# Thirty-two matmuls of ones and the identity between the last norm's sums and the spread of its result

## The chip, the cores and the metric

The kernel runs on one core of a Trainium2 chip. The metric is the device time of one execution in microseconds (us), and less is better. Five engines take part: TensorE (PE, with its weight loads listed apart as PEld), VectorE (DVE), ScalarE (ACT), GpSimd (POOL) and SyncE (SP), the last of which issues most of the transfers (DMAs) from the memory of the chip.

## The reference

The input is one sequence of 512 frames with 1024 channels in float32. Two layers each do

```
x = x + 0.5 * swiglu(rms_norm(x, ffn1_norm), ffn1_w_in, ffn1_w_out)
x = x + hybrid_mixer(rms_norm(x, mix_norm), ...)   # conv | stick-breaking | retention
x = x + 0.5 * swiglu(rms_norm(x, ffn2_norm), ffn2_w_in, ffn2_w_out)
```

and after the second layer stands the last norm, with which the change has to do:

```
def rms_norm(x, g):
    y = x * lax.rsqrt(jnp.mean(x * x, axis=-1, keepdims=True) + 1e-6)
    return y * g
```

## The kernel before, in words

The activations lie transposed: eight tiles `x[d]` of 128 channels by 512 frames. Matrix products in float32 are made from matmuls in a reduced format (`F32R`): every operand is split into a high and a low part, and each product takes three matmuls (lines 432 to 434, and 658 to 660 for a scheme of blocks that needs seven block products for eight). Weights come from memory as raw tiles of 512 KB (`load`, line 387), ACT copies the high part (line 374), DVE subtracts it for the low part (line 377); some weights are split with the help of an accumulating DMA from POOL instead.

The order of the work is not written out by hand. Every operation is put on a list with an engine, a planned cost, its dependencies and a shift named `late`. A planner (`Plan.forward`) then steps through a planned time: whenever an engine is free, it takes the operation that is ready and has the lowest rank, where the rank is the operation's place on the list plus `late`. The resulting order is emitted, and on the chip each engine works through its own instructions in that order. Several shifts are given by name and by kind of stage (`SHIFTS`); in the first stage all that `weight` does, the loads of raw weights included, carries a shift of -1015. Only the order comes from the planned costs; on the chip the instructions wait for semaphores. On-chip buffers are taken from rooms with a fixed number of places; the banks of `mm` are three.

The start of the program (`run`, from line 1327 on) puts on the list, one after another: the load of the gains (`const`, line 1341), a small memset, `warm` (ten matmuls of zeros, line 600), then the loads of the `x[d]` (line 1355) with pieces of the first weights (`first_weights`, line 582) between them. The first product (lines 432 to 434, tile `pf`) needs the first `x` scaled by its gain (line 465) and a piece of the first weights.

The end is the last norm, `norm(self.y, True)`, and is a chain in which each step waits for the one before:

- ACT squares the last `x[d]` (line 474). The other squares were added up by DVE before.
- `sums` (line 551): TensorE sums the squares over the channels, eight small matmuls for the last `sq`, into the bank `ss`.
- `inv_sqrt`: DVE scales and adds the epsilon (line 488, tile `ms`), POOL raises to the power of -1/2 (line 495, tile `rt`).
- `spread`: DVE lays the 512 results on diagonals (line 518, tile `dg`), and TensorE multiplies them by ones, in full float32, into the bank `bc` (line 537). In the trace this matmul is two instructions.
- DVE multiplies each `x[d]` by gain and `bc` (line 1413), and SP sends the eight results out (line 1418).

## Time and profile before

| | |
|---|---|
| median of 3 runs | 1920.43 us (1914.89, 1920.43, 1923.8) |
| the profiled execution's own time | 1916.82 us |
| its span, from the first to the last instruction | 1915.1 us |
| TensorE busy (PE) | 1884.7 us, 98% of the span |
| weight loads (PEld) | 1683.5 us, 88% |
| VectorE, ScalarE, GpSimd busy | 69%, 50%, 12% |
| mean granted TensorE clock | 0.995 |
| read from memory | 288.98 MB |

The profile is one execution. In a timeline each row gives the start, the time from the first start to the last end of a merged group, the engine, the line of the program, the operation with its tiles (output, arrow, inputs), and behind `x` how many instructions were merged; in square brackets stands how long the engine had been idle and what ended that. A row of windows gives for a stretch of time the busy time of each engine with the number of instructions, the granted TensorE clock as a part of full speed (PEclk), the busy share of the DMA engines, and their rate. In the chain that ended last, each row is a start, a length and what the end of the program hung on in that time. The records of matmuls overlap, since matmuls are pipelined; the distance between two starts says how fast they follow each other.

### The profile page before, as it was taken

Reading aid. Unit: us, or ns where it says so; the run is one execution under the profiler, and the core shown is the slowest. Engines: PE = TensorE matmul, PEld = TensorE weight load, DVE = VectorE, ACT = ScalarE, POOL = GpSimd, SP = SyncE. Lnnn points to the kernel's source line nnn. Section 1 sums busy time; section 2 is a strip of 40 time slices with the busy share of each in tenths; the row PEclk is TensorE's granted clock in tenths of the full one; section 3 lists DMA queues with packets and bytes.
Section 4 is the critical chain, followed back from the end, with each engine's and each line's share of the span. In section 5 each row is a group of like instructions: output and inputs, shape, how many; then the busy total and the mean of one; then the engine's idle time right before and its main releaser. Section 6 shows DMA issues by size and latency. Waiting matters only on the chain.

```text
span 1915.1 us, 28971 instructions
## 1 busy us (share of the span) xinstructions
PE 1884.7 (98%) x11412; PEld 1683.5 (88%) x11412; DVE 1326.1 (69%) x1921; ACT 963.6 (50%) x1527; POOL 226.2 (12%) x262
## 2 busy tenths in 40 slices
PE   9999999999999999999999999999999999999997
PEld 7899999888878889899889999998888889998995
DVE  6865656699787856566685656657987887564665
ACT  5444444455886534343554444444668855353442
POOL 1011010011101010110211010100111020110100
PEclk9999999999999999999999999999999999999998
DMA  8457665465347577676866675655554385675742
GB/s 249 121 155 181 179 170 152 137 163 125 94 93 188 136 178 190 166 187 167 213 145 170 166 198 163 176 141 142 132 136 120 76 216 140 167 207 153 188 136 78
DMA packets 106343, 301.35 MB, mean 157 GB/s; under 512 B 12384, under 2 KB 13920, under 8 KB 106208
## 3 DMA queue, kind: packets, MB, share of 16 engines
q0 software_dynamic: 43520, 112.74, 30.6%
q1 hardware_dynamic: 62688, 186.78, 30.0%
q8 instruction: 89, 1.46, 0.3%
q14 instruction: 46, 0.38, 0.1%
HBM read 288.98 MB, written 2.10 MB: 152 GB/s over the span
## 4 chain that ended last, share of the span: by engine, by line
PE 81%; DVE 7%; DMA 7%; issue 2%; ACT 2%; SPq 0%; POOL 0%; POOLq 0%; DVEq 0%; ACTq 0%
PE po L432 8%; PE po L433 8%; PE po L434 8%; PE pu L658 6%; PE pu L660 6%; PE pu L659 6%; DMA w_raw<-in_f_in 5%; PE pr L660 4%; PE pr L658 4%; PE pr L659 4%; PE pf L432 4%; PE pf L433 4%; PE pf L434 4%; DVE yc L1198 2%; PE mo L433 2%
## 5 line engine op out<-in xcount | busy, mean ns | idle before, releaser
L377 DVE TENSOR_TENSOR w_lo<-w_raw,w_hi 128x1024 fp32r<-128x1024 f32 (+2 forms) x281 | 313.3, 1116 | 170.4 <-PE po L434 58.6
L374 ACT CAST w_hi<-w_raw 128x1024 fp32r<-128x1024 f32 (+2 forms) x281 | 269.6, 963 | 240.2 <-DMA w_raw<-in_f_in 71.9
L432 PE MATMUL po<-hh,w_hi 128*128 128x512 f32 x704 | 275.8, 392 | 0.3 <-DVE x L777 0.3
L433 PE MATMUL po<-hl,w_hi 128*128 128x512 f32 x704 | 275.4, 391 | 0.0
L434 PE MATMUL po<-hh,w_lo 128*128 128x512 f32 x704 | 273.9, 389 | 0.0
L658 PE MATMUL pr<-T_hi,s_hi 128*128 128x256 f32 x560 | 158.2, 282 | 2.6 <-ACT ga L695 2.6
L658 PE MATMUL pu<-B_hi,w_hi 128*128 128x256 f32 x560 | 158.5, 283 | 2.0 <-DVE up L708 1.9
L659 PE MATMUL pu<-B_lo,w_hi 128*128 128x256 f32 x560 | 158.4, 283 | 0.0
L660 PE MATMUL pu<-B_hi,w_lo 128*128 128x256 f32 x560 | 158.2, 283 | 0.0
L659 PE MATMUL pr<-T_lo,s_hi 128*128 128x256 f32 x560 | 158.2, 282 | 0.0
L660 PE MATMUL pr<-T_hi,s_lo 128*128 128x256 f32 x560 | 158.1, 282 | 0.0
L434 PEld LDWEIGHTS po<-hh,w_lo 128*128 128x128 f32 x704 | 132.2, 188 | 28.6
L432 PEld LDWEIGHTS po<-hh,w_hi 128*128 128x128 f32 x704 | 132.5, 188 | 24.4 <-DVE x L777 1.2
L433 PEld LDWEIGHTS po<-hl,w_hi 128*128 128x128 f32 x704 | 132.7, 188 | 22.2
L673 POOL DMA_DIRECT2D w_raw<-in_f_in x70 | 84.0, 1209 | 573.9 <-DMA w_raw<-in_f_in 409.3
L777 DVE SCALAR_TENSOR_TENSOR x<-po,x 128x512 f32<-128x512 f32 x128 | 87.0, 686 | 54.6 <-PE po L434 54.1
L402 ACT ACTIVATE w_lo<-w_hi 128x1024 fp32r<-128x1024 f32 (+2 forms) x85 | 79.3, 932 | 89.1 <-DMA w_hi<-in_f_out 19.6
L432 PE MATMUL pf<-xh,w_hi 128*128 128x512 f32 x304 | 119.1, 392 | 0.0
L434 PE MATMUL pf<-xh,w_lo 128*128 128x512 f32 x304 | 118.5, 390 | 0.0
L433 PE MATMUL pf<-xl,w_hi 128*128 128x512 f32 x304 | 118.4, 390 | 0.0
L721 ACT ACTIVATE ga<-ga 128x512 f32<-128x512 f32 x88 | 55.4, 630 | 120.2 <-DVE ga L715 109.3
L695 ACT COPY ga<-pr 128x256 f32<-128x256 f32 x140 | 51.7, 370 | 126.5 <-PE pr L660 125.8
(216 smaller groups left out, 5034.5 us busy)
## 6 DMA issues: line engine op xcount, KB each, us to landing
w_raw<-in_f_in SPq DMA_DIRECT2D x225, 512.0 KB, 4.6
w_raw<-in_f_in POOLq DMA_DIRECT2D x70, 512.0 KB, 7.8
w_raw<-in_f_out SPq DMA_DIRECT2D x48, 320.0 KB, 3.3
w_raw<-in_f_out SPq DMA_DIRECT2D x38, 384.0 KB, 4.0
w_raw<-in_m_in SPq DMA_DIRECT2D x26, 512.0 KB, 4.3
w_hi<-in_f_out POOLq DMA_DIRECT2D x26, 384.0 KB, 4.4
w_lo<-in_f_out POOLq DMA_DIRECT2D x26, 384.0 KB, 5.0
w_hi<-in_f_in POOLq DMA_DIRECT2D x19, 512.0 KB, 6.3
```

Of the source, the lines that this page charges most:

```text
L374: self.a(n, lambda: nc.scalar.copy(view(hi), view(src)), [src], [hi])
L377: lambda: nc.vector.tensor_tensor(out=view(lo), in0=view(src), in1=view(hi).bitcast(F32), op=ALU.subtract),
L402: self.a(n, lambda: nc.scalar.activation(lo[:, :n], hi[:, :n].bitcast(F32), ACT.Copy, scale=-1.0), [hi], [lo])
L432: mm(acc[:], hi[:, c], h[:], start=first and a + i == 0, stop=False)
L433: mm(acc[:], hi[:, c], l[:], start=False, stop=False)
L434: mm(acc[:], lo[:, c], h[:], start=False, stop=last and a + i == len(ks) - 1)
L658: mm(out, hi[:, c], h, start=first and j + i == 0, stop=False, **opts)
L659: mm(out, hi[:, c], l, start=False, stop=False, **opts)
L660: mm(out, lo[:, c], h, start=False, stop=j + i == 2, **opts)
L673: lambda: nc.gpsimd.dma_start(rs[:].rearrange("p (a b) -> p a b", a=2), src[:, None, 2 * q : 3 * q].to_broadcast([P, 2, q]), accum_op=ALU.add,
L721: self.last_silus = [self.a(S, lambda: nc.scalar.activation(g[:], g[:], ACT.Silu), [g], [g], "silu")]
L777: lambda x=x, po=po: nc.vector.scalar_tensor_tensor(out=x[:], in0=po[:], scalar=-0.5, in1=x[:], op0=ALU.mult, op1=ALU.add),
```

## The change

The change has four parts, all on what the program emits or on what the planner believes:

- `norm`, when it is the last, calls a new function `keep(8, ...)` after the sums. It takes a bank named `kept` from the room `mm` and emits 32 matmuls of 128 columns with `ones_r` as the weights and `ident_r` as the moving operand. Nobody reads the bank. The planner is told that the operation comes after the last sums.
- The load of the gains moves behind the load of `x[0]` on the list, and carries the shift `FIRST`, -20000.
- The planned cost of one matmul of `warm` goes from 0.6 to 0.5 us. The ten matmuls stay.
- Loads of the first weights and of `x` may carry the same shift up to a number `EARLY`. With `EARLY = 0` neither condition (`j < EARLY`, `d < 2 * EARLY - 1`) is met by any of them.

```
+FIRST, EARLY = -20000, 0
...
             self.pe(0.225 * TT, sums, [sq, self.ones], [ps])
+        if last:
+            self.keep(8, len(self.plan.ops) - 1)
         self.r = self.inv_sqrt(ps, TT, 1.0 / D)
         bc = self.spread(self.r, room, "bc", 1 if last else 2)
...
-        self.pe(0.6 * n, fn, [t], [ps])
+        self.pe(0.5 * n, fn, [t], [ps])
+
+    def keep(self, n, sums):
+
+        ps = self.bank(self.mm, "kept")
+
+        def fn():
+            for i in range(4 * n):
+                self.nc.tensor.matmul(ps[:, :P], self.ones_r[:], self.ident_r[:], start=i == 0, stop=i == 4 * n - 1)
+
+        self.pe(0.24 * n, fn, [self.ones_r, self.ident_r], [ps]).deps.add(sums)
...
-        gains = const("gains", [P, 3 * DEPTH + 1, KT])
-        g = [Col(gains, i) for i in range(3 * DEPTH + 1)]
         self.x = [self.tile(self.f2, f"x{d}") for d in range(KT)]
...
-            self.dma(262144, lambda: nc.sync.dma_start(x[:], io["x"][:, d, :]), [], [x])
+            self.dma(262144, lambda: nc.sync.dma_start(x[:], io["x"][:, d, :]), [], [x], FIRST if d < 2 * EARLY - 1 else 0)
...
+        load_x(0)
+        gains = const("gains", [P, 3 * DEPTH + 1, KT], late=FIRST)
+        g = [Col(gains, i) for i in range(3 * DEPTH + 1)]
...
         for j in range(4):
-            load_x(2 * j)
+            if j:
+                load_x(2 * j)
```

## The prediction

> **What bounds the kernel now.** I read the page first: the share of each engine, the granted clock, the chain that ended last.

> ```profile
> span 1915.1 us, 28971 instructions
> PE 1884.7 (98%) x11412; PEld 1683.5 (88%) x11412; DVE 1326.1 (69%) x1921; ACT 963.6 (50%) x1527; POOL 226.2 (12%) x262
> PEclk9999999999999999999999999999999999999998
> PE 81%; DVE 7%; DMA 7%; issue 2%; ACT 2%; SPq 0%; POOL 0%; POOLq 0%; DVEq 0%; ACTq 0%
> ```

> TensorE is busy for all but 30.4 us (1915.1 - 1884.7) and carries 81% of the chain. What is put behind its work, or delays its first product, therefore reaches the end one for one. The clock is whole in every slice but the last. So I went to the last 15 us, where the new matmuls go, with the timeline and then with windows of 1 us.

> ```profile
> 1899.62 0.69 DVE L777 SCALAR_TENSOR_TENSOR x<-po,x 128x512 f32<-128x512 f32 x1 [2.12 <-PE po L434]
> ...
> 1901.03 1.05 PE L551 MATMUL ss<-ones,sq 128*128 128x1 f32 x8 [1.45 <-ACT sq L474]
> 1902.12 0.16 DVE L488 TENSOR_SCALAR ms<-ss 128x4 f32<-128x4 f32 x1 [1.81 <-PE ss L551]
> 1902.43 1.04 POOL L495 TENSOR_TENSOR rt<-ms,mhalf 128x4 f32<-128x4 f32 x1 [34.50 <-DVE ms L488]
> 1903.50 0.69 DVE L518 TENSOR_TENSOR dg<-c_ident,rt 128x512 f32<-128x512 f32 x1 [1.22 <-POOL rt L495]
> ...
> 1904.34 2.05 PE L537 MATMUL bc<-dg,ones 128*128 128x512 f32 x2 [2.26 <-DVE dg L518]
> 1906.42 0.75 DVE L1413 SCALAR_TENSOR_TENSOR o<-x,c_gains,bc 128x512 f32<-128x512 f32 x1 [2.23 <-PE bc L537]
> ```

> ```profile
> 1903.00:1904.00 1.00, 0.00 (x0) 0.00 (x0) 0.50 (x1) 0.00 (x0) 0.47 (x1) 0.91 0.00 0
> 1904.00:1905.00 1.00, 0.66 (x1) 0.50 (x2) 0.19 (x1) 0.00 (x0) 0.00 (x0) 0.50 0.00 0
> 1905.00:1906.00 1.00, 1.00 (x2) 0.00 (x0) 0.00 (x0) 0.00 (x0) 0.00 (x0) 0.50 0.00 0
> ```

> The sums end at 1902.08. TensorE then has nothing until 1904.34, while DVE, POOL and DVE work. In that pause the clock falls to a half (0.91 of the third window: (1 - 0.91) / 0.5 = 0.18 us of it are low, so it fell near 1903.82), and `bc` runs for 2.05 us at the half clock. The eight `o` wait for it, and the outputs for them. The pause and the slow `bc` are all that the new matmuls can touch.

> **Part 1: the 32 matmuls.** They stand behind the sums and ahead of `bc` in TensorE's queue; `bc` is the only instruction behind them. How fast do they follow each other? The nearest rows are eight matmuls of the same size, with the same identity moving, and two of the same size in the scores:

> ```profile
> 508.84 0.22 PE L935 MATMUL z<-qh,kk 128*128 128x128 f32 x1
> 508.90 0.27 PE L935 MATMUL z<-ql,kk 128*128 128x128 f32 x1
> ...
> 511.49 1.00 PE L1129 MATMUL rbc<-ident_r,ex 128*128 128x128 f32 x8
> 512.33 0.45 PE L432 MATMUL pj<-xh,w_hi 128*128 128x512 f32 x1
> ```

> From the first of the eight to what comes after them are 0.84 us, so 0.105 us each; the pair stands 0.06 apart. I take 0.105: it is a run of eight with its weight loads, and 32 of them are a run too; 0.06, seen between two alone, is the lower bound. The matmul after the eight began 0.16 us before their end (511.49 + 1.00 - 512.33), so the first new one can begin at 1902.08 - 0.16 = 1901.92. 32 x 0.105 = 3.36 us, and `bc` begins at 1905.28 instead of 1904.34: 0.94 us later.

> What does `bc` gain? TensorE would now be busy from 1901.03 on, so I take the clock to stay whole. The same float32 product, 512 wide and in two instructions, at full clock:

> ```profile
> 497.54 1.02 PE L1102 MATMUL yce<-yr,c_centre 128*128 128x512 f32 x2
> ```

> So `bc` ends at 1906.30, and DVE starts 0.03 us behind it as before (1904.34 + 2.05 = 1906.39 against 1906.42): 1906.33, a gain of 0.09 us. What the clock gives, the queue takes back. Break-even is (1905.37 - 1901.92) / 32 = 0.108 us for one matmul; nothing is lost in the queue below (1904.34 - 1901.92) / 32 = 0.076. The price lies so near the break-even that the sign of this term is open, its size is not. Bounds: -1.03 us at 0.06 (rival 1), +2.04 us if the clock falls all the same (rival 2).

> [...]

> The bank costs no wait: the last reader of any `po` bank, the row at 1899.62, is done 1.6 us before. The operands are constants of the start. Nothing waits for the result.

> **Part 2: the gains go first.** SP's queue at the start, and the chain there:

> ```profile
> 0.74 0.86 SPq L387 DMA_DIRECT2D w_raw<-in_f_in  x2
> ...
> 1.64 0.43 SPq L1341 DMA_DIRECT2D c_gains<-in_gains  x1
> 2.12 0.47 SPq L1355 DMA_DIRECT2D x<-in_x  x1
> ```

> ```profile
> 1.18 4.98 DMA w_raw<-in_f_in
> ...
> 6.18 1.00 ACT w_hi L374
> ...
> 7.24 0.72 ACT xh L465
> 7.96 0.30 ACT wf_hi L374
> ...
> 8.30 0.50 PE pf L432
> ```

> Before, the two raw loads go ahead of the gains, since their rank carries -1015. With -20000 the gains pass both; `x[0]`, which is moved on the list as well, keeps a rank above theirs and stays fourth. The first three issues only change places, so `x[0]` still goes at 2.12 and all behind it as before. But the chain runs through the second raw load: it is issued one place later, 2.12 - 1.64 = 0.48 us. Its cast on ACT stands ahead of `xh`, which follows it at once, so the first product begins at 8.78. From there TensorE runs without a pause, so this term is +0.48 us. Lower bound 0, if the memory and not the issue sets when the load lands; below nothing only by the clock (next). 0.48 is the nearest row, and I take it.

> The clock has its own phase at the start:

> ```profile
> 9.00:10.00 1.00, 1.00 (x4) 0.70 (x4) 1.00 (x4) 1.00 (x3) 0.00 (x0) 0.71 1.07 381
> ...
> 12.00:13.00 1.00, 1.00 (x4) 0.78 (x3) 0.89 (x2) 1.00 (x4) 0.00 (x0) 0.59 1.00 365
> ```

> ```profile
> 10.13 0.43 PE pf L433
> ...
> 14.20 0.23 PE pf L433
> ```

> Some 3.4 us (0.58 and 0.82 us in these two windows, 2 between) run at half clock, a product of 0.23 us taking 0.43. That is 3.4 x (1 - 0.23 / 0.43) = 1.6 us which another execution may have or not: it widens the range by 1.6 us each way.

> **Part 3: `warm` at 0.5 us in the plan; `EARLY = 0`.** The matmuls stay, and on the chip TensorE idles between them and the first product:

> ```profile
> 1.46 4.63 PE L600 MATMUL warm<-zeros 128*128 128x512 f32 x10 [1.46 <-DVE mhalf L1358]
> 8.30 0.50 PE L432 MATMUL pf<-xh,wf_hi 128*128 128x512 f32 x1 [2.21 <-ACT wf_hi L374]
> ```

> A planned end that is 1 us earlier gives TensorE nothing that is ready, so I cost it at nothing; what hides it is the wait for `wf_hi`. `EARLY = 0` shifts no load: nothing.

> **Sum.** +0.48 - 0.09 = +0.39 us. Against the profiled execution: 1916.82 + 0.39 = 1917.2 us. That execution lies 3.6 us below the median of the three runs, and all four spread over 8.9 us, so I centre on their mean, 1918.99: 1919.4 us.

> **The rivals.**

> 1. *The pause holds the new matmuls.* At 0.06 us each they end at 1903.84, `bc` starts at 1904.34 as before and ends at 1905.36: -1.03 us, with the start 1918.99 - 1.03 + 0.48 = 1918.4 us. For it speaks the pair in the scores; against it the run of eight.

> 2. *The clock falls all the same.* If matmuls 128 wide do not count as work enough, 18 are done by 1903.82; below, a matmul goes from 0.12 to 0.21 us at the low clock, so the other 14 take 0.184 each, `bc` starts at 1906.4 and takes 2.05. DVE starts near 1908.46: +2.04 us, in all 1921.5 us. The change would then not do what it is for. [...]

> 3. *The other side: the planner writes another order, and loads come late.* In the plan the first raw loads start one place of SP later. The room of raw tiles has two places, so the third load waits for the split of the first and may lose its turn to a constant; each later pick of the planner depends on what is ready, and a swap at the start can be carried on. What one late load costs, this trace shows once in the first stage:

> ```profile
> PE pr L658 <- ACT ga L695: 2.2, 1, 2.2
> ```

> ```profile
> 150.39 0.12 PE pr L658
> ...
> 152.70 10.54 DMA w_raw<-in_f_in
> ...
> 166.93 0.21 PE pr L658
> ```

> ```profile
> 166.00:168.00 2.00, 1.86 (x9) 1.86 (x10) 2.00 (x4) 0.64 (x2) 0.00 (x0) 0.61 0.74 124
> 168.00:170.00 2.00, 2.00 (x12) 2.00 (x11) 2.00 (x3) 1.08 (x2) 0.00 (x0) 0.54 0.89 316
> ```

> A load of 10.54 us stops TensorE for 2.2 us, and 3.4 us of half clock follow (1.56 and 1.84 in the two windows), worth 3.4 x (1 - 0.12 / 0.21) = 1.5: 3.7 us. From three more such stalls on (11.1 us, 1930.5 us) the change is slower by more than 0.5%. Against it: all loads from `x[0]` on keep their place, and once TensorE is the bound a shift of all times alike changes no pick.

> 4. *The same, the other way*: an order that loses its stalls. Of TensorE's 30.4 us of idle time, 8.7 come after `bc`, 2.26 and 1.45 before it, 3.7 at the start; some 14 remain, of which 9.6 would have to go. About 1909 us.

> **How the numbers follow.** 0.5% is 9.6 us, about what a measurement of this kernel can tell from no change. The forecast has 0.64, rival 1 0.10, rival 2 0.08: all three lie within 2.5 us of the time before, so 0.82 for the same. Rival 3 has 0.12 and rival 4 0.06. The range: from the lowest run, less rival 1 (1.0), the clock at the start (1.6) and part of one stall, 1911; upward from the highest, plus 0.5, 2.0 and 1.6, 1928, and to 1930 to meet rival 3.

> **What the next profile would show.** On TensorE one group of 32 `kept` matmuls from about 1901.9 (plus the shift of the start), 3.4 us long; the clock at 1.00 until `bc` ends; `bc` x2 in 1.02 us, and DVE's first `o` within 0.2 us of where it was, counted from the sums' end. Distances near 0.06 show rival 1, a clock of 0.5 over `bc` rival 2. At the start the gains ahead of both raw loads, and the first product near 8.8. A plan that is unchanged shows the same groups and counts on every engine but for TensorE's 32; other stalls of TensorE, or changed splits of the work, show rivals 3 or 4. The prediction is wrong if the order moves: nothing in the two terms themselves can reach 9.6 us.

## The result, and the profile after

| | before | after |
|---|---|---|
| median of 22 runs each | 1920.43 us (1914.89 to 1928.61) | 1929.5 us (1924.64 to 1933.14) |
| the profiled execution's own time | 1916.82 us | 1925.42 us |
| its span | 1915.1 us | 1923.7 us |

The ratio is 1.0038, with a 95% interval from 1.003 to 1.0047: slower by about 7.3 us (5.8 to 9.0); the two medians lie 9.07 us apart. The median lies in the predicted range, near its upper end, and the step is smaller than the 0.5% that the forecast counted as no change. But the interval excludes no change: the term of the tail came out with the other sign and many times its size, and the planner's order, which the sum left out, cost as much again. Only the term of the gains came out about as forecast.

The page of the changed kernel hardly tells the two apart: the same counts on every engine but TensorE (32 more), the clock whole in every slice but the last, a chain that is TensorE's.

```profile
span 1923.7 us, 29021 instructions
PE 1891.6 (98%) x11444; PEld 1689.9 (88%) x11444; DVE 1326.7 (69%) x1921; ACT 965.3 (50%) x1527; POOL 226.4 (12%) x262
PEclk9999999999999999999999999999999999999998
PE 84%; DVE 7%; DMA 6%; ACT 2%; issue 1%; SPq 1%; DVEq 0%; ACTq 0%; POOLq 0%
```

**Where the 8.6 us of span are.** TensorE does the same matmuls in both kernels, so one can follow a tile by its k-th matmul. The tile `bc` of the norms gives the first and the last of twelve such points, before and then after (times are those of the first and the last start):

```profile
L537 PE MATMUL bc<-dg,ones_r x12: 392/393/500, 33.1 to 1562.4; 128*128 128x512 f32 x12
```

```profile
L539 PE MATMUL bc<-dg,ones_r x12: 392/393/505, 34.3 to 1567.3; 128*128 128x512 f32 x12
```

After lags by 1.2 us at 33 us and by 4.9 us at 1562 us. Matched matmul by matmul, the lag jumps to 8.59 us near 50 us, falls to 4.61 us near 170 us, wanders between 3.0 and 5.4 us from there, is 5.38 us at the last sums and 8.6 us at the end. So there are two losses, one in the first 60 us and one behind the last sums, and a part of the first is given back. Of the 1.2 us at 33 us, 0.6 are the later first product. The rest goes with the half clock of the start, where the products begin 0.43 us apart: it ends at 14.26 here and at 12.88 before, but at 14.42 in e1, which has the order of before, so it is not the change that moves it. (The clock's record of this trace begins at 14.25 us, so that its window rows show a whole clock ahead of that.)

**The tail.** The timeline of the changed kernel, with the windows of the same stretch (columns as in the prediction; the value behind POOL is the granted clock):

```profile
1906.41 1.05 PE L553 MATMUL ss<-ones,sq 128*128 128x1 f32 x8 [1.45 <-ACT sq L476]
...
1907.32 5.86 PE L616 MATMUL kept<-ident_r,ones_r 128*128 128x128 f32 x32
...
1908.88 0.69 DVE L520 TENSOR_TENSOR dg<-c_ident,rt 128x512 f32<-128x512 f32 x1 [1.22 <-POOL rt L497]
...
1912.98 2.02 PE L539 MATMUL bc<-dg,ones 128*128 128x512 f32 x2
1915.04 5.36 DVE L1430 SCALAR_TENSOR_TENSOR o<-x,c_gains,bc 128x512 f32<-128x512 f32 x8 [5.46 <-PE bc L539]
```

```profile
1907.00:1908.00 1.00, 1.00 (x11) 1.00 (x11) 0.16 (x1) 0.00 (x0) 0.19 (x1) 1.00 0.06 16
1908.00:1909.00 1.00, 1.00 (x10) 1.00 (x9) 0.12 (x1) 0.00 (x0) 0.85 (x1) 0.83 0.00 0
1909.00:1910.00 1.00, 1.00 (x7) 1.00 (x6) 0.57 (x1) 0.00 (x0) 0.00 (x0) 0.50 0.00 0
```

`dg` is ready at 1909.57, but `bc` starts at 1912.98, behind the last `kept`. TensorE is busy without a gap, and the clock falls all the same, near 1908.66 ((1 - 0.83) / 0.5 = 0.34 us of that window are low). Up to there the new matmuls begin about 0.11 us apart (12 of them from 1907.32 to 1908.58), then 0.21 (20 from 1908.71 to 1912.77); the numbers in round brackets also count a matmul that reaches into the window from the one ahead. `bc` gets the half clock after all: 2.02 us. From the start of the last sums to the first `o` were 5.39 us before (1906.42 - 1901.03); now 8.63: 3.24 us lost.

**The start.** The gains go first, `x[0]` is still issued at 2.12, and the first product begins 0.61 us later than before (8.91 against 8.30):

```profile
0.74 0.38 SPq L1357 DMA_DIRECT2D c_gains<-in_gains  x1
1.18 0.90 SPq L389 DMA_DIRECT2D w_raw<-in_f_in  x2
2.12 0.43 SPq L1368 DMA_DIRECT2D x<-in_x  x1
```

```profile
8.91 0.80 PE L434 MATMUL pf<-xh,wf_hi 128*128 128x512 f32 x1 [2.78 <-ACT wf_hi L376]
```

The large loss comes 40 us later. First the waits of the changed kernel from 38 to 60 us (engine, what waited for what: total, times, longest), in which before has no wait of TensorE, then VectorE's and TensorE's rows:

```profile
DVE up L738 <- ACT ga L737: 6.4, 2, 6.2
...
PE pf L436 <- DVE w_lo L379: 4.5, 1, 4.5
```

```profile
40.68 1.05 ACT L376 CAST w_hi<-w_raw 128x1024 fp32r<-128x1024 f32 x1 [5.12 <-DMA w_raw<-in_f_in]
...
43.71 0.69 DVE L738 TENSOR_TENSOR up<-up,ga 128x512 f32<-128x512 f32 x1 [6.22 <-ACT ga L737]
...
48.12 1.22 DVE L379 TENSOR_TENSOR w_lo<-w_raw,w_hi 128x1024 fp32r<-128x1024 f32 x1
...
49.39 0.79 PE L436 MATMUL pf<-xh,w_lo 128*128 128x512 f32 x1 [4.46 <-DVE w_lo L379]
```

```profile
48.00:50.00 2.00, 0.61 (x2) 0.51 (x3) 2.00 (x4) 0.00 (x0) 0.00 (x0) 0.60 0.00 0
50.00:52.00 2.00, 2.00 (x6) 1.61 (x5) 2.00 (x6) 1.97 (x3) 0.00 (x0) 0.50 0.68 240
52.00:54.00 2.00, 2.00 (x6) 1.52 (x6) 1.05 (x1) 1.17 (x2) 0.00 (x0) 0.50 0.06 23
54.00:56.00 2.00, 2.00 (x8) 1.57 (x7) 1.90 (x3) 1.54 (x2) 0.58 (x1) 0.70 0.82 240
```

The same low part in the kernel before:

```profile
38.79 1.23 DVE L377 TENSOR_TENSOR w_lo<-w_raw,w_hi 128x1024 fp32r<-128x1024 f32 x1 [6.30 <-ACT w_hi L374]
```

The high part of this tile of weights (`w_hi`) is cast at 40.68, 3.0 us later than before (37.70). Its low part came 1.1 us behind the cast before; now it comes 7.4 us behind, since VectorE's order has put the gate's `ga`, `up` and `hl` ahead of it, and `up` waits 6.22 us for ScalarE. TensorE stands for 4.46 us. Then the clock is low for 6.8 us (1.6 + 2 + 2 + 1.2, each from the row's clock), of which TensorE works some 5.8 at half speed: 4.5 + 2.9 = 7.4 us, which is the jump from 1.2 to 8.59. At 164.0 us before has the stall that the prediction quotes, 2.2 us and 3.4 us of half clock (2.2 + 1.7 = 3.9); after has none there, and the lag falls by 3.98 us. So the new order trades one wait for a dearer one. Of the 3.9 us only the wait belongs to the order: in e1, e5 and e6, which have the order of before there, the same wait takes 1.4 to 1.6 us and the clock stays whole.

Drawn again from the planners of the two kernels, the order differs at 105 of VectorE's 1921 places, 78 of ScalarE's 1519, 96 of TensorE's 1990 (the 32 matmuls aside), 15 of SP's 484 and 12 of POOL's 258, and all but one of these lie in the first 196 planned us. The planner's first pick moved: the gains take SP's first place. Read from the planned times, the first two raw loads slip one place, the second's split on VectorE slips behind others, and the fourth raw load finds its buffer at 16.3 instead of 13.6 planned us. The fifth lands later in turn, and its low part, the one of the rows above, due at 34.0, loses its turn to the gate's steps of lower rank and is planned for 40.25.

### The profile page after: what moved, and what is told of

Its sections match the earlier page's. It is cut to its first block, busy times and chain, and to the rows that moved or that the text cites. A ratio compares the mean times of both kernels' runs of the same rounds, so it can differ in the third digit from the quotient of the medians.

```text
span 1923.7 us, 29021 instructions
## 1 busy us (share of the span) xinstructions
PE 1891.6 (98%) x11444; PEld 1689.9 (88%) x11444; DVE 1326.7 (69%) x1921; ACT 965.3 (50%) x1527; POOL 226.4 (12%) x262
## 4 chain that ended last, share of the span: by engine, by line
PE 84%; DVE 7%; DMA 6%; ACT 2%; issue 1%; SPq 1%; DVEq 0%; ACTq 0%; POOLq 0%
PE po L434 8%; PE po L435 8%; PE po L436 8%; PE pu L674 6%; PE pu L676 6%; PE pu L675 6%; PE pr L676 5%; PE pr L675 5%; PE pr L674 5%; DMA w_raw<-in_f_in 4%; PE pf L436 3%; PE pf L434 3%; PE pf L435 3%; DVE yc L1214 2%; PE mo L435 2%; PE mo L434 2%
## 5 line engine op out<-in xcount | busy, mean ns | idle before, releaser
L434 PE MATMUL po<-hh,w_hi 128*128 128x512 f32 x704 | 276.0, 392 | 0.3 <-DVE x L793 0.3
L434 PEld LDWEIGHTS po<-hh,w_hi 128*128 128x128 f32 x704 | 132.5, 188 | 24.7 <-DVE x L793 1.2
L434 PE MATMUL pf<-xh,w_hi 128*128 128x512 f32 x304 | 120.1, 395 | 0.0
```

The source lines that it names most:

```text
L434: mm(acc[:], hi[:, c], h[:], start=first and a + i == 0, stop=False)
```

## The experiments

Two theories stood against each other for the tail (the 32 cost their place in the queue; the clock falls because TensorE idles, or because these matmuls do not count as work) and two for the start (the order on SP alone; the planner's order on VectorE and ScalarE).

**e1, the 32 matmuls alone**, on the kernel before; all other orders are those of before.

```
+        if last:
+            self.keep(8, len(self.plan.ops) - 1)
...
+    def keep(self, n, sums):
...
```

> The kernel before with only the 32 matmuls added; the order of every engine is that of before but for them. Theory (the tail and the start are two separate losses): the stretch from the start of the last sums to the end of bc grows from 5.4 us (1901.03 to 1906.39) to about 8.6 us as in the changed kernel (1906.41 to 1915.00), the start stays as before, so +3.2 us in all, a ratio near 1.0017. Rival (the matmuls alone make the whole loss): +7 to +9 us, ratio 1.004. Rival (the tail of the changed kernel was an unlucky moment of the clock): within 1 us of before, ratio 1.000, and bc in 1.02 us.

Measured: 1.0030, interval 1.0013 to 1.0046; median 1928.1 us.

```profile
1911.79 1.42 PE L551 MATMUL ss<-ones,sq 128*128 128x1 f32 x8 [1.45 <-ACT sq L474]
...
1913.08 7.07 PE L612 MATMUL kept<-ident_r,ones_r 128*128 128x128 f32 x32
...
1919.94 2.02 PE L537 MATMUL bc<-dg,ones 128*128 128x512 f32 x2
1921.99 3.38 DVE L1425 SCALAR_TENSOR_TENSOR o<-x,c_gains,bc 128x512 f32<-128x512 f32 x5 [6.67 <-PE bc L537]
```

```profile
1912.00:1913.00 1.00, 1.00 (x8) 1.00 (x7) 0.00 (x0) 0.00 (x0) 0.00 (x0) 0.66 0.00 0
```

The tail takes 10.20 us (1921.99 - 1911.79). The clock falls at 1912.32, within the sums and ahead of the first `kept`, and all 32 run at the half clock: (1919.94 - 1913.08) / 32 = 0.214 us each. The matmuls alone make the kernel slower, and 32 of them do not bring the clock back within 6.9 us. The interval holds the 1.0017 of the theory and the 1.004 of the rival alike, so this time does not decide between them; e2's does. This execution is 10.8 us behind before's already at the last sums (1911.79 against 1901.03), with the same order up to there: so much can two executions differ by chance late in the program, and only the rows of one stretch are compared here, not whole spans.

**e2, all but the 32**: the changed kernel without its call of `keep`.

```
-        if last:
-            self.keep(8, len(self.plan.ops) - 1)
```

> The changed kernel without the 32 matmuls; all else, the planned order included, as in the change. Theory (two separate losses): TensorE stalls again for about 4.5 us near 45 us, waiting for a low part from DVE, with 6.8 us of half clock behind it, and the time is 3 to 6 us above before, ratio 1.0015 to 1.003. Rival (the matmuls alone): same as before, ratio 1.000. Rival (the stall was of one execution): no stall near 45 us, ratio 1.000.

Measured: 1.0029, interval 1.0012 to 1.0047; median 1927.27 us. The wait is there, and longer:

```profile
PE pf L436 <- DVE w_lo L379: 6.4, 1, 6.4
```

```profile
46.00:48.00 2.00, 0.00 (x0) 0.00 (x0) 2.00 (x3) 1.75 (x3) 0.00 (x0) 0.50 0.00 0
...
56.00:58.00 2.00, 2.00 (x10) 1.64 (x9) 2.00 (x4) 0.77 (x2) 0.92 (x1) 0.94 0.61 170
```

From 46.0 to 56.24 the clock is low. The lag behind before is 9.5 us from 50 to 150 us and 5.5 us from 200 to 400 us. Each half of the change is slower by itself. Their sum, 0.59%, is more than the whole's 0.38%, but with about 0.17% of uncertainty on either half this says nothing on whether they add up.

**e3, SP's order alone.** The plan of before, but in what is emitted the gains stand first and the one constant that the changed kernel issues ahead of the next raw load stands there too; VectorE, ScalarE, POOL and TensorE keep their order.

```
         order = self.order()
+        order.remove(self.ops[0])
+        order.insert(0, self.ops[0])
+        order.remove(self.ops[74])
+        order.insert(order.index(self.ops[124]), self.ops[74])
```

> The kernel before, its plan untouched, but emitted with SP's two swaps of the changed kernel: gains ahead of the first two raw loads, c_tri ahead of the third raw load. DVE, ACT, POOL and TensorE have the order of before. Theory (what costs is the order on DVE and ACT that the planner draws from the swap): at most 0.5 us at the first product, no stall near 45 us, ratio within 1.0005. Rival (the later loads themselves are what starves TensorE): a stall of 2 to 5 us near 45 us as in the changed kernel, ratio 1.002 to 1.003.

Measured: 0.9992, interval 0.9979 to 1.0005; median 1920.72 us. Of the wait near 50 us 1.4 us are left, although the low part is as late as its load makes it, 41.25 against 38.79 before:

```profile
PE pf L438 <- DVE w_lo L381: 1.4, 1, 1.4
```

```profile
41.25 1.23 DVE L381 TENSOR_TENSOR w_lo<-w_raw,w_hi 128x1024 fp32r<-128x1024 f32 x1 [6.29 <-ACT w_hi L378]
```

So loads that are some 2.5 us late cost little as long as VectorE splits them at once; e7, with all of SP's order as before, has a wait of 1.2 us at the same place too. SP's swaps are not the cause by themselves. (The changed kernel has five more exchanges of SP's places, which this run leaves out; they are planned for 123 us and later, behind the wait near 50.)

**e4, one place on VectorE.** e2 with the low part (operation 140 of the list) put back ahead of the gate's first product with the silu (operation 235, the row `up<-up,ga`).

```
         order = self.order()
+        order.remove(self.ops[140])
+        order.insert(order.index(self.ops[235]), self.ops[140])
```

> The changed kernel without the 32 matmuls, and one DVE instruction moved: the subtraction that makes the low part of the second half of the weights of the fourth product (it stood seventh, behind the products with the silu and two other low parts) goes ahead of the first product with the silu. Theory (DVE's order makes the stall): the stall of 4.5 us near 45 us and its 6.8 us of half clock go; 5 to 7.5 us less than without that move, so 1 to 4 us below before if nothing else becomes late. Rival (the load lands late whatever the order): the low part is still after 45 us, the stall stays above 2 us, the time is within 2 us of the kernel without the move.

Measured: 1.0001, interval 0.9984 to 1.0018; median 1922.64 us against 1927.27 of e2. The old wait is gone, but half of it comes back at the next split, which stands behind on ScalarE as well as on VectorE:

```profile
PE pf L436 <- ACT w_hi L378: 2.5, 1, 2.5
PE pf L438 <- DVE w_lo L381: 0.7, 1, 0.7
```

The clock is low for 6.8 us here too, from 51.4 us on, and the 1 to 4 us below before that were expected did not come.

**e8, three places.** e4 with the next split put forward as well, its cast on ScalarE (142) and its low part (143).

```
+        for o, at in ((140, 235), (142, 244), (143, 244)):
+            order.remove(self.ops[o])
+            order.insert(order.index(self.ops[at]), self.ops[o])
```

> The changed kernel without the 32 matmuls, with the DVE instruction moved as before, and with the next pair of weights' parts (the cast on ACT and its low part on DVE) put ahead of the third product's scaling and silu. Theory (the order on DVE and ACT makes the stalls of TensorE near 45 to 52 us): what is left of them is under 1.5 us, the loss at 100 us against before is under 3 us, ratio 0.998 to 1.000. Rival (the loads land too late in this order of SP, whatever DVE and ACT do): stalls of 2.5 us or more remain there.

Measured: 0.9987, interval 0.9976 to 0.9998; median 1918.17 us. One wait of half a microsecond remains, and the clock is whole from 42 to 58 us:

```profile
PE pf L439 <- DVE w_lo L382: 0.5, 1, 0.5
```

```profile
48.00:50.00 2.00, 1.48 (x7) 1.13 (x7) 2.00 (x5) 0.63 (x1) 0.00 (x0) 1.00 0.24 27
```

Three instructions out of some 29,000 put back, and the loss of e2 is gone, all of it. That settles the cause at the start: the planner's order on VectorE and ScalarE, not the loads. That e8 comes out a little below before fits the trace: it keeps the part of the new order that has no stall at 164.0 us.

**e5, fewer of the same**: twenty narrow matmuls instead of 32, on the kernel before.

```
+            self.keep(5, len(self.plan.ops) - 1)
```

> The kernel before with 20 of the narrow matmuls (128 columns) in place of 32. At full clock they last 20 x 0.105 = 2.1 us and would fit the pause of 2.3 us. Theory (a narrow stream with a weight load for each matmul does not hold the clock, so it halves in or ahead of the pause): the clock is at 0.5 over bc, the 20 matmuls take 2.8 to 4.3 us, bc 2.0 us; from the start of the last sums to the first output 6.4 to 8 us, against 5.4 to 6.2 without. Rival (32 were only too many): the clock stays whole, bc takes 1.02 us, the stretch is 4.4 to 4.6 us.

Measured: 1.0011, interval 0.9998 to 1.0024. The clock fell at 1907.6, with the sums, so this trace shows twenty at the half clock:

```profile
1908.74 4.51 PE L612 MATMUL kept<-ident_r,ones_r 128*128 128x128 f32 x20
1913.05 2.02 PE L537 MATMUL bc<-dg,ones 128*128 128x512 f32 x2
```

Tail: 7.81 us. The price goes by the number of matmuls at the low pace (4.31 us for 20, 0.216 each), not by a fixed wait; whether fewer would keep the clock, it cannot say.

**e6, wide matmuls.** Ten of 512 columns (the identity read four times) instead of 32 of 128, on the kernel before.

```
+        def fn():
+            out = ps[:].rearrange("p (a b) -> p a b", b=P)
+            wide = self.ident_r[:, None, :].to_broadcast([P, TT, P])
+            for i in range(n):
+                self.nc.tensor.matmul(out, self.ones_r[:], wide, start=i == 0, stop=i == n - 1)
```

> The kernel before with ten matmuls of 512 columns after the sums (2.3 us at full clock) in place of the 32 of 128: the same engine busy for the same time, but its array streaming most of it. [...] Rival (busy is what counts, width does not matter): like 20 narrow ones.

Measured: 1.0014, interval 1.0001 to 1.0027. The clock still falls, and comes back while `bc` runs.

```profile
1912.00:1913.00 1.00, 1.00 (x4) 0.73 (x4) 0.16 (x1) 0.00 (x0) 0.80 (x1) 0.72 0.00 0
...
1915.00:1916.00 1.00, 1.00 (x2) 0.05 (x1) 0.00 (x0) 0.00 (x0) 0.00 (x0) 0.58 0.00 0
1916.00:1917.00 1.00, 0.30 (x1) 0.00 (x0) 0.66 (x1) 0.00 (x0) 0.00 (x0) 1.00 0.00 0
```

It is low from 1912.44 to 1915.84 (0.56 + 1 + 1 + 0.84 = 3.4 us) and whole again, still within `bc`, which takes 1.58 us. The tail takes 5.98 us, no better than without any. The timed runs are 0.14% slower than before, which this one tail does not explain; that stays open.

**e7, wide ones on both sides**: six more in TensorE's pause ahead of the last sums, ten behind them.

```
+            if last and i:
+                self.keep(6, max(o.i for o in self.plan.ops if o.engine == "tensor" and o.i not in own))
...
+        if last:
+            self.keep(10, len(self.plan.ops) - 1)
```

> The kernel before with six matmuls of 512 columns ahead of the last sums, while TensorE waits for the last square, and ten after them. [...]

Measured: 1.0009, interval 0.9996 to 1.0022; median 1923.35 us. In the trace the clock stays whole to the end of `bc`, which takes 1.10 us:

```profile
1908.53 1.56 PE L616 MATMUL kept<-ident_r,ones_r 128*128 128x512 f32 x6
...
1910.14 1.05 PE L553 MATMUL ss<-ones,sq 128*128 128x1 f32 x8
...
1911.05 2.54 PE L616 MATMUL kept<-ident_r,ones_r 128*128 128x512 f32 x10
...
1913.45 1.10 PE L537 MATMUL bc<-dg,ones 128*128 128x512 f32 x2
1914.59 5.36 DVE L1429 SCALAR_TENSOR_TENSOR o<-x,c_gains,bc 128x512 f32<-128x512 f32 x8 [1.28 <-PE bc L537]
```

The tail is 4.45 us, the shortest seen, 0.9 to 1.8 us less than without. The twelve timed runs cannot resolve a gain of that size: their ratio lies above 1, and the interval allows a gain as well as a loss.

**e9, e8 and e7 together.**

> The two repairs together: the changed kernel's order with the moved instructions on DVE and ACT (three instructions), and wide matmuls on both sides of the last sums in place of the 32 narrow ones. Theory: the start as with the moves alone (under 1.5 us of stalls near 45 to 52 us), the tail from the sums to the first output 4.4 to 4.6 us at a clock of 1.00 against 5.4 to 6.2 us without the wide matmuls, so 1 to 1.5 us below the moves alone: ratio 0.998 to 0.9985 against the kernel before. Rival (the wide matmuls held the clock by a lucky phase): the clock at 0.5 over bc in this execution, the stretch 7 us or more, ratio above 0.999.

Measured: 0.9988, interval 0.9972 to 1.0003; median 1919.31 us, before on that chip 1922.66.

```profile
1901.33 1.05 PE L558 MATMUL ss<-ones,sq 128*128 128x1 f32 x8
1902.25 2.54 PE L623 MATMUL kept<-ident_r,ones_r 128*128 128x512 f32 x10
...
1904.64 1.10 PE L542 MATMUL bc<-dg,ones 128*128 128x512 f32 x2
1905.78 5.36 DVE L1437 SCALAR_TENSOR_TENSOR o<-x,c_gains,bc 128x512 f32<-128x512 f32 x8 [1.28 <-PE bc L542]
```

The tail repeats at 4.45 us, with the clock at 1.00 from 1901 to 1906 us. Against the changed kernel both losses are gone. Against before no gain is shown beyond that of e8, whose interval is the only one that ends below 1; the 1 to 1.5 us that were expected on top of e8 are not seen.

## Why the prediction was wrong

**Part 1, the clock.** The step that failed is "TensorE would now be busy from 1901.03 on, so I take the clock to stay whole". It was busy and the clock fell. Counted from the start of the last sums, `bc` was to begin after 4.25 us and take 1.02; it began after 6.57 and took 2.02. The term of -0.09 us measured +3.24 in the profiled execution. Over the traces at hand, the tail takes 8.63 and 10.20 us with the 32 (after, e1) and 5.39, 6.21, 5.95, 5.70 and 6.21 without (before, e2, e3, e4, e8): +3.5 us between the means. That is outside the bounds too. Rival 2 named the outcome. Its price of +2.04 was too low for two reasons: it took 0.184 us at the low pace, where 0.214 was measured, and it took the fall for as late as before, after 18 of the 32, where it came after 12 (after) or before the first (e1). And the width alone is not why the clock fell: in e6 it fell as well, near 1912.44, with ten wide ones in the place of the 32. What makes it fall no run here shows; what passed around the falls stands in the last section.

The pace of 0.105 us was a little short as well. In the row of eight the first two begin 0.06 us apart and the others 0.11 (511.49, 511.55, 511.66, 511.77 and so on), and a run of 32 goes by the 0.11, as the distances in after up to the fall show. That lies above the break-even of 0.108: even with the clock whole the term would have been a loss of some 0.2 us (an estimate: the 32 begin 0.91 us behind the start of the sums, 0.14 + 31 x 0.112 = 3.61 us to `bc`, 1.02 for it and 0.04 to the first `o` make 5.58, against 5.39).

**Part 2, the gains.** Right in size: +0.48 us expected at the first product, +0.61 measured in after. Over all traces it begins at 8.70 to 8.94 with the gains first (after, e2, e3, e4, e8, e9) and at 8.24 to 8.50 in the order of before (before, e1, e5, e6, e7), 0.43 us between the means. It was a trifle beside what the same edit did through the planner. The 1.6 us of half clock at the start, which another execution "may have or not", are in all eleven traces; only their end moves, from 11.9 to 14.6 us.

**Rival 3.** It happened, and had 0.12. The step that failed is "once TensorE is the bound a shift of all times alike changes no pick". The shift was not alike: SP's later places kept their planned times while one split slipped by 2.7 planned us, and the order of all five engines came out new in the first 196 planned us. And its price was built for three stalls of 3.7 us each. The one that came cost 7.4 us (after) and 9.5 (e2), since TensorE stood longer, and half clock lasts for two or three stretches of 3.4 us instead of one. Rival 4 came true in part: the stall at 164.0 us went, worth 3.9 us in this execution of before, of which 1.7 are a half clock that e1, e5 and e6 do not have. Net of it, e2's trace keeps 5.5 us.

**Part 3** was right: with only the cost of `warm` changed, the emitted order is that of before, and `EARLY = 0` moves nothing. The bank cost no wait.

**The size of the effect against the measurement.** The prediction took 9.6 us as about what a measurement can tell and put everything within it together as no change. With 22 runs of each, 1.6 us either way could be told, and two losses of some 3.5 and 5 us add up to more than that.

## What to carry to other kernels

In two traces (e7, e9), with six wide matmuls ahead of the last sums and ten behind them, TensorE's clock stayed at 1.00 over the pause, `bc` took 1.10 us, and the tail 4.45 us, 0.9 to 1.8 us less than without; the timed runs are too few to show that it pays. With ten wide ones behind the sums alone it fell (e6: 3.4 us at 0.50, `bc` in 1.58 us). Such matmuls also cost their places in the queue: 32 narrow ones took 0.11 us each at the full clock and 0.21 at the half. Where a planner draws the order from planned times, look at an edit's emitted order on every engine before believing that it is local: a shift of one place among the planner's first picks, 0.33 planned us, cost 7.4 us on the chip, in part given back later. What a late operand costs here is the wait, and behind waits of 2.2 to 6.4 us also 3.4 to 10.24 us of half clock (before, after, e2, e4; none behind the 1.4 us of e3 and the 0.5 us of e8); three instructions put back by hand can test that.

## What the runs showed of the hardware

The last 3.41 us ahead of the fall in after, and the 3.41 us behind it:

```profile
1905.24:1908.65 3.41, 2.24 (x20) 2.24 (x21) 0.61 (x2) 0.63 (x1) 0.84 (x1) 1.00 0.02 5
1908.65:1912.07 3.42, 3.42 (x18) 3.42 (x18) 0.69 (x1) 0.00 (x0) 0.20 (x1) 0.50 0.00 0
```

The same length behind the fall in e6, where the clock comes back at its end:

```profile
1912.43:1915.85 3.42, 3.42 (x9) 2.05 (x7) 0.69 (x1) 0.00 (x0) 0.37 (x1) 0.50 0.00 0
```
